# Two Strassen groups in the first FFN of an encoder kernel, with the tokens normalised in its middle

## The chip, the cores and the metric

The kernel runs on one core of a Trainium2 chip. The metric is device microseconds of one execution; the time of a version is the median of its runs. One execution is also taken with the hardware profiler, and all rows below come from that one. TensorE (PE) multiplies, VectorE (DVE) and ScalarE (ACT) do elementwise work, GpSimd (POOL) a few tiny things, and SP issues nearly all transfers from memory (DMA).

## The reference, cut to what matters

256 tokens of width 1024 go through two layers. Each layer is FFN, token mixing, FFN, every one with a norm before and after. All is float32.

```python
def rms_norm(x, g):
    xf = x * rsqrt(mean(x * x, axis=-1) + 1e-6)
    return xf * g

def swiglu(h, w_up, w_down):            # w_up 1024 x 5632, w_down 2816 x 1024
    a, b = split(h @ w_up, 2, axis=-1)
    return (silu(a) * b) @ w_down

for l in range(2):
    h = rms_norm(x, ffn1_pre_g[l])
    x = x + 0.5 * rms_norm(swiglu(h, ffn1_w_up[l], ffn1_w_down[l]), ffn1_post_g[l])
    x = x + rms_norm(mix(rms_norm(x, mix_pre_g[l]), mem, positions), mix_post_g[l])
    h = rms_norm(x, ffn2_pre_g[l])
    x = x + 0.5 * rms_norm(swiglu(h, ffn2_w_up[l], ffn2_w_down[l]), ffn2_post_g[l])
```

The mixing needs, among others, a cosine and sine table of the positions, a lambda from four small vectors, and memory tokens `mem`, normalised.

## The kernel before, in words

**Numbers in two parts.** A float32 matmul is made of three matmuls on parts: each operand is a high part (a rounded copy) and a low part (the rest). Products are high x high, high x low, low x high. Tokens and weights are both split so. For weights this is `split_unit` (lines 113 to 125): ScalarE copies the high part `wh` (line 119), VectorE subtracts to get the low part `wl` (line 120), each in two halves (four in the first five units of a stage).

**Units.** Weights lie in memory as units of 128 x 2048 floats, 1 MB, in the order of their use. SP loads them one after the other into five `raw` buffers; five `wh` and five `wl` buffers take the split ones. So loading and splitting run ahead of TensorE by as much as these buffers allow.

**An FFN** has 11 pairs, each 256 columns of the gate half and 256 of the value half of the up-weights. `up_both(p)` (`u` in the plan) takes two units and makes 48 matmuls of 128x512, 24 for each of the two token blocks (c = 0, 1) of 128 tokens. `swiglu` turns the bank into the hidden values, `turned` transposes them on TensorE (line 325) and splits them (lines 164, 165). `down(p)` (`d`) multiplies them by one unit of down-weights, 24 matmuls into the accumulators `acc` (line 277).

**A Strassen group** `group(p)` (`g`, line 384) makes two pairs together: four raw units w11, w12, w22, w21 (gate and value columns, upper and lower 512 rows), seven products of 12 matmuls on sums of weights (VectorE adds whole units, line 366) and sums of tokens (`token_sums`, line 374, from unsplit copies `kept` of the turned tokens). That is 84 matmuls instead of 96 for two plain pairs. VectorE and ScalarE split seven units instead of four.

**The plan** (line 37) is the order of an FFN, after pairs 0 and 1 and before the last three down-products. The second line is for the three later FFNs; the first line is for the first FFN, which has no groups: its tokens come raw. The host passes x also transposed, `first_tokens` multiplies it by the gain only, and the scale of each token, 1 / rms, is put on in `swiglu` (lines 337, 338). So the first product can start before the rms is known. Later stages get normalised tokens from `pre_norm` (line 187), whose `turn` transposes them (line 207) and splits them; copies go to `kept`.

**Other work inside the first FFN.** `ahead` (line 881), called after the sixth step of its plan (d2), runs `setup` (rope tables, lambda products; three small transfers, some 25 small VectorE operations, three sines), `mem_scale` (four transfers of mem, four squares, two scales) and `mem_gain` (four transfers of the transposed mem, split into the tile that the mixing reads). In layer 1 `ahead` runs `mem_gain` alone, after the whole plan.

**What sets the order.** The program is written in order of use, and a list scheduler places instructions on each engine: the earliest in the program that it takes to be ready goes next, and buffers are given out as earlier users release them. On the chip each engine keeps the order that was fixed then, and so does SP's queue of transfers. Pools that the change touches: `xhl` (split tokens, 2 buffers), `hid` (12), `s2` (8 of 128x512: swiglu values, kept tokens, setup's tables), `s4` (2), `gain` (2), and two banks each for `ma` and `mb`.

Of the kernel before, what the change touches and what calls it, by code (L numbers as in the profile page):

```python
# [9 lines left out]
F32 = mybir.dt.float32  # L10
F32R = mybir.dt.float32r
# [3 lines left out]
ALU = mybir.AluOpType  # L15
AX = mybir.AxisListType

P = 128
D = 1024
# [15 lines left out]
T_ROPE = 13  # L35
T_SC = (242, 336)
PLAN = [[(t[0], int(t[1:])) for t in plan.split()] for plan in (
    "u2 d0 u3 d1 u4 d2 u5 d3 u6 d4 u7 d5 u8 d6 u9 d7 u10",
    "u2 d0 g3 d1 d2 u5 d3 g6 d4 d5 u8 d6 g9 d7",
)]  # L40
T_KT = (200, 222)
# [10 lines left out]
def encoder_kernel(ctx, tc, x_d, xt_d, mem_d, memt_d, pos_d, w_d, gains_d, cols_d, lamv_d, poolw_d, cst_d, out_d):  # L52
    nc = tc.nc
# [20 lines left out]
    def mb_bank():  # L74
        return mmp.tile([P, 512], F32, name="mb")

    def t2(shape=(P, 512), dt=F32):
        return s2.tile(list(shape), dt, name="s2")
# [11 lines left out]
    def gain(row):  # L90
        g = gbp.tile([P, D], F32, name="gain")
        nc.sync.dma_start(out=g, in_=gains_d[row].partition_broadcast(P))
        return g
# [69 lines left out]
    def split(ps, h, l):  # L163
        high = nc.scalar.copy(out=h, in_=ps)  # L164
        return high, nc.vector.tensor_tensor(out=l, in0=ps, in1=h.bitcast(F32), op=ALU.subtract)  # L165
# [19 lines left out]
        return [gained_split((xx[0][:, c, 4 * b + k, :], xx[1][:, c, 4 * b + k, :]), t[:, k, :], colt[:, cols[k]:cols[k] + 1]) for k in range(4)]  # L185

    def pre_norm(c, src, g, xx, keep):
        xh, xl, _ = xx
        xn = s4.tile([P, D], F32, name="s4")

        def gained(var):
            for b in range(2):
                fs = slice(b * 512, (b + 1) * 512)
                issue_after([nc.vector.tensor_tensor(out=xn[:, fs], in0=src[b], in1=g[:, fs], op=ALU.mult)], var)

        r = rstd_of(src, 1.0, gained)
        for b in range(2):
            fs = slice(b * 512, (b + 1) * 512)
            nc.vector.tensor_scalar(out=xn[:, fs], in0=xn[:, fs], scalar1=r, scalar2=None, op0=ALU.mult)

        def turn():
            tps = []
            for b in range(2):
                ps = mb_bank()
                for k in range(4):
                    i = 4 * b + k
                    tps.append(nc.tensor.transpose(out=ps[:, k * P:(k + 1) * P], in_=xn[:, i * P:(i + 1) * P], identity=ident))  # L207
                pv = ps.rearrange("p (k t) -> p k t", t=P)
                split(pv, xh[:, c, b * 4:b * 4 + 4, :], xl[:, c, b * 4:b * 4 + 4, :])
                if keep is not None:  # L210
                    keep[c, b] = t2()
                    nc.scalar.copy(out=keep[c, b], in_=ps)
            return tps

        return turn

    def post_norm(c, banks, g, half_step):
        ts = [t2(), t2()]
# [77 lines left out]

    def ffn(i, xx, late, kept, g_post, finish, ahead, raw_rstd=None):
        fine[0] = FINE
        hid = {}
        acc = [[None, None], [None, None]]  # L300

# [31 lines left out]

        def swiglu(p, c, ps):
            sg, hn = t2((P, S)), t2((P, S))
            if raw_rstd:
                nc.scalar.activation(out=sg, in_=ps[:, 0:S], func=AF.Silu, scale=raw_rstd[c])
                nc.vector.scalar_tensor_tensor(out=hn, in0=ps[:, S:2 * S], scalar=raw_rstd[c], in1=sg, op0=ALU.mult, op1=ALU.mult)
            else:
                nc.scalar.activation(out=sg, in_=ps[:, 0:S], func=AF.Silu)  # L340
                nc.vector.tensor_tensor(out=hn, in0=ps[:, S:2 * S], in1=sg, op=ALU.mult)
            turned(hn, c, [p])
# [8 lines left out]
        def up_both(p):  # L351
            ws = (next_unit(), next_unit())
            for c in range(2):
                up(p, c, ws, leave=1 - c)
                if kept and p == 2 and c == 0:
                    token_sums()

        def product(out, at, w, first=True, last=True):
# [6 lines left out]
        def add(out, a, b):  # L365
            nc.vector.tensor_tensor(out=out, in0=a, in1=b, op=ALU.add)  # L366

        if kept:
            sums = xts.tile([P, 2, 4 * 4, P], F32R, name="xhl")

            def summed(j):
                return lambda k: (sums[:, 0, 4 * j + k, :], sums[:, 1, 4 * j + k, :])

        def token_sums():
            a11, a12, a21, a22 = (kept[c, b] for c in range(2) for b in range(2))
            s1 = t2()
            nc.vector.tensor_tensor(out=s1, in0=a22, in1=a21, op=ALU.subtract)
            nc.vector.tensor_tensor(out=a21, in0=a11, in1=a21, op=ALU.subtract)
            nc.vector.scalar_tensor_tensor(out=a11, in0=s1, scalar=-1.0, in1=a11, op0=ALU.mult, op1=ALU.subtract)
            nc.vector.scalar_tensor_tensor(out=a12, in0=a11, scalar=-1.0, in1=a12, op0=ALU.mult, op1=ALU.subtract)  # L380
            for j, t in enumerate((s1, a11, a21, a12)):
                split(t.rearrange("p (k t) -> p k t", t=P), sums[:, 0, 4 * j:4 * j + 4, :], sums[:, 1, 4 * j:4 * j + 4, :])
# [47 lines left out]
            for c in range(2):  # L430
                swiglu(p, c, banks[c])

        if raw_rstd:
            ws = [(next_unit(), next_unit())]
            hs, ls = first_high, first_low
            (ha, la), (hb, lb), (hc, lc), (hd, ld) = (zip(*late[c, b]) for b in range(2) for c in range(2))
            in_order([*ha, *hs[0:4], *hb, *hc, hs[4], hs[5], *hd, *hs[6:8]])
            in_order([*la, *ls[0:4], *lb, *lc, ls[4], ls[5], *ld, *ls[6:8]])
            ws.append((next_unit(), next_unit()))
            for c in range(2):  # L440
                rstd_of(halves(x[c]), 1.0, None, raw_rstd[c])
            up_first(0, ws[0])
            for c in range(2):
                up(1, c, ws[1], acc_bank)
        else:
            ws = [(next_unit(), next_unit()) for _ in range(2)]
            done = []
            for c in range(2):
                for p in range(2):
                    done += up(p, c, ws[p], acc_bank if c else ma_bank, 2)  # L450
            issue_after(late, done[T_UP])
        for n, (what, p) in enumerate(PLAN[bool(kept)]):
            if what == "d":
                down(p)
            elif what == "u":
                up_both(p)
            else:
                group(p)
            if not kept and n == 5:
                ahead()  # L460
        if kept:
            ahead()
        todo = [(next_unit(), p) for p in range(NPR - 3, NPR)]
        return tail(acc, todo, lhs_of, 0, NPR - 1, g_post, True, finish, flush)

# [103 lines left out]
    def mem_scale():  # L569
        for c in range(2):  # L570
            m = []
            for b in range(2):
                t = hids.tile([P, 512], F32, name="hid")
                nc.sync.dma_start(out=t, in_=mem_d[c * P:(c + 1) * P, b * 512:(b + 1) * 512])
                m.append(t)
            rstd_of(m, 1.0, None, rmem[:, c:c + 1])
# [269 lines left out]
    cur = xt_pair()  # L846
# [17 lines left out]
    kept = None  # L864
    for i, (kind, l, row) in enumerate(stages):
        nx = {}

        def finish(c):
            if i + 1 == len(stages):
                for b in range(2):  # L870
                    fs = slice(b * 512, (b + 1) * 512)
                    nc.sync.dma_start(out=out_d[c * P:(c + 1) * P, fs], in_=x[c][:, fs])
                return []
            if c == 0:
                nx["xx"] = xt_pair()
                nx["kept"] = {} if stages[i + 1][0] == "ffn" else None
                nx["g"] = gain(stages[i + 1][1] * 10 + stages[i + 1][2])
            return pre_norm(c, halves(x[c]), nx["g"], nx["xx"], nx["kept"])()

        if kind == "ffn":  # L880
            def ahead():
                if i == 0:
                    setup()
                    mem_scale()
                if row == 0:
                    nx["mem"] = mem_gain(l)

            late = ffn(i, cur, late, kept, gain(l * 10 + row + 1), finish, ahead, [rst[:, c:c + 1] for c in range(2)] if i == 0 else None)
        else:
            late = mix(l, cur, late, mem, finish)  # L890
        cur, mem, kept = nx.get("xx"), nx.get("mem"), nx.get("kept")
# [24 lines left out]
def _pack(a, np):  # L916
# [17 lines left out]
    def ffn(up, down, first):  # L934
        def pair(p):
            wide(up, np.r_[256 * p:256 * p + 256, D_FF + 256 * p:D_FF + 256 * p + 256])

        pair(0)
        pair(1)
        for what, p in PLAN[not first]:  # L940
            if what == "d":
                rows(down, p)
            elif what == "u":
                pair(p)
            else:
                for half, col in ((0, 0), (0, D_FF), (1, D_FF), (1, 0)):
                    block(up, half, 256 * p + col)
        for p in range(NPR - 3, NPR):
            rows(down, p)
# [59 lines left out]
```

## Time and profile before

| | |
|---|---|
| median of 3 runs | 1119.22 us (1118.71 to 1120.41) |
| the profiled execution | 1118.06 us, its span 1116.0 us |
| instructions | 13913 |
| TensorE clock granted | 0.998 of full speed |
| HBM read | 216.33 MB |

The stages in the profile, by the first matmul of each: first FFN 6 us, mixing 194, second FFN of layer 0 384, first FFN of layer 1 563, mixing 742, last FFN 932. A row of the timeline gives start, length, engine, line, operation, output <- inputs, shape and count; brackets hold the idle time of that engine just before and what ended it. PE is a matmul, PEld a load of weights into TensorE. Matmuls overlap, so the steps between their starts tell more than their lengths.

### The profile page before, as it was taken

What the parts mean: (1) busy time and instruction counts of PE and PEld (TensorE: products, weight loads), DVE (VectorE), ACT (ScalarE), POOL (GpSimd) and SP (SyncE); (2) the same over time, 40 slices, a digit from 0 to 9 for tenths busy, and PEclk for the clock granted to TensorE, in tenths of its full rate; (3) what the DMA queues carried; (4) which work ended last, traced back from release to release, by engine and by line L of the source; (5) the groups of instructions that cost most, each with busy time, mean ns of one, the idle gap of its engine ahead of it and who ended that gap; (6) DMA issues with size and microseconds to landing.
All of it is one profiled execution on the core that took longest, in us unless ns stands there. A gap on an engine that the chain in (4) does not pass through costs nothing.

```text
span 1116.0 us, 13913 instructions
## 1 busy us (share of the span) xinstructions
PE 1106.6 (99%) x5247; PEld 912.6 (82%) x5247; DVE 892.5 (80%) x1215; ACT 651.6 (58%) x1082; POOL 25.5 (2%) x37
## 2 busy tenths in 40 slices
PE   9999999999999999999999999999999999999997
PEld 6888888888888888888888888888888888888886
DVE  6767456657858899999989999995676678999994
ACT  7657345546575557474675674765566637575571
POOL 0000000000000100000000000010000001000000
PEclk9999999999999999999999999999999999999999
DMA  9966643564563454573851835565445645273731
GB/s 344 396 225 230 216 150 125 189 226 150 201 214 134 174 203 140 200 251 131 334 196 69 302 125 214 207 250 207 171 170 191 236 155 177 90 255 137 287 113 38
DMA packets 35489, 218.27 MB, mean 196 GB/s; under 512 B 4192, under 2 KB 4448, under 8 KB 11232
## 3 DMA queue, kind: packets, MB, share of 16 engines
q1 hardware_dynamic: 35424, 217.40, 53.6%
q8 instruction: 41, 0.67, 0.2%
q14 instruction: 24, 0.20, 0.0%
HBM read 216.33 MB, written 1.05 MB: 195 GB/s over the span
## 4 chain that ended last, share of the span: by engine, by line
PE 95%; DMA 2%; ACT 1%; DVE 1%; POOL 0%; issue 0%; SPq 0%; DVEq 0%; POOLq 0%; ACTq 0%
PE ma L235 52%; PE acc L277 24%; PE mb L235 9%; PE acc L235 5%; PE mb L325 2%; PE mb L207 1%; PE acc L664 1%; PE acc L687 1%; PE mb L564 1%; DMA hid<-in_memt 1%; DMA hid<-in_xt 1%; PE acc L750 1%; DMA raw<-in_w 0%; POOL sm L148 0%; PE acc L734 0%; DVE wl L120 0%
## 5 line engine op out<-in xcount | busy, mean ns | idle before, releaser
L120 DVE TENSOR_TENSOR wl<-raw,wh 128x1024 fp32r<-128x1024 f32 (+1 forms) x498 | 523.5, 1089 | 96.6 <-ACT wh L119 94.2
L119 ACT CAST wh<-raw 128x1024 fp32r<-128x1024 f32 (+1 forms) x498 | 444.4, 947 | 196.1 <-DVE raw L366 67.4
L235 PE MATMUL ma<-wh,xhl 128*128 128x512 f32 x1664 | 530.1, 393 | 0.1
L235 PEld LDWEIGHTS ma<-wh,xhl 128*128 128x128 f32 x1664 | 311.7, 188 | 65.5 <-issue 1.7
L235 PE MATMUL ma<-wl,xhl 128*128 128x512 f32 x832 | 327.1, 393 | 0.4 <-DVE wl L120 0.2
L277 PE MATMUL acc<-wh,hid 128*128 128x512 f32 x704 | 227.8, 395 | 0.0
L235 PEld LDWEIGHTS ma<-wl,xhl 128*128 128x128 f32 x832 | 156.4, 188 | 33.0 <-DVE wl L120 1.3
L277 PEld LDWEIGHTS acc<-wh,hid 128*128 128x128 f32 x704 | 132.2, 188 | 26.9
L277 PE MATMUL acc<-wl,hid 128*128 128x512 f32 x352 | 136.8, 390 | 0.0
L235 PE MATMUL mb<-wh,xhl 128*128 128x512 f32 x280 | 90.5, 389 | 0.0
L366 DVE TENSOR_TENSOR raw<-raw 128x2048 f32<-128x2048 f32 x36 | 82.2, 2284 | 0.4
L277 PEld LDWEIGHTS acc<-wl,hid 128*128 128x128 f32 x352 | 66.3, 188 | 12.7
L235 PEld LDWEIGHTS mb<-wh,xhl 128*128 128x128 f32 x280 | 52.6, 188 | 10.9
L235 PE MATMUL mb<-wl,xhl 128*128 128x512 f32 x140 | 54.5, 389 | 0.0
L235 PE MATMUL acc<-wh,xhl 128*128 128x512 f32 x160 | 51.6, 391 | 0.0
L340 ACT ACTIVATE s<-ma 128x256 f32<-128x256 f32 x24 | 8.9, 386 | 65.6 <-PE ma L235 65.2
L148 POOL TENSOR_TENSOR sm<-sm,mhalf 128x1 f32<-128x1 f32 (+1 forms) x26 | 22.6, 868 | 1002.3 <-DVE sm L157 822.8
L277 PE MATMUL acc<-wh,xhl 128*128 128x512 f32 x128 | 40.7, 394 | 0.0
L155 ACT ACTIVATE junk<-acc 128x512 bf16<-128x512 f32 x24 | 14.3, 597 | 44.1 <-PE acc L277 44.1
L164 ACT CAST hid<-mb 128x256 fp32r<-128x256 f32 x88 | 32.1, 370 | 13.1 <-PE mb L325 10.6
L165 DVE TENSOR_TENSOR hid<-mb,hid 128x256 fp32r<-128x256 f32 x88 | 36.3, 417 | 1.8 <-ACT hid L164 1.3
L235 PEld LDWEIGHTS acc<-wh,xhl 128*128 128x128 f32 x160 | 30.0, 188 | 6.2
(161 smaller groups left out, 880.5 us busy)
## 6 DMA issues: line engine op xcount, KB each, us to landing
raw<-in_w SPq DMA_DIRECT2D x189, 1024.0 KB, 4.8
gain<-in_gains SPq DMA_DIRECT2D x17, 512.0 KB, 4.7
raw<-in_w SPq DMA_DIRECT2D x8, 256.0 KB, 5.7
hid<-in_memt SPq DMA_DIRECT2D x8, 256.0 KB, 6.5
hid<-in_xt SPq DMA_DIRECT2D x4, 256.0 KB, 5.4
raw<-in_w SPq DMA_DIRECT2D x2, 512.0 KB, 7.0
x<-in_x SPq DMA_DIRECT2D x4, 256.0 KB, 6.6
hid<-in_mem SPq DMA_DIRECT2D x4, 256.0 KB, 9.3
```

What stands on the lines that cost most here:

```text
L119: high = nc.scalar.copy(out=h[:, cs], in_=raw[:, cs])
L120: low = nc.vector.tensor_tensor(out=l[:, cs], in0=raw[:, cs], in1=h.bitcast(F32)[:, cs], op=ALU.subtract)
L148: nc.gpsimd.tensor_tensor(out=r, in0=v, in1=mhalf[:, :n], op=ALU.pow)
L155: sq.append(nc.scalar.activation(out=junk, in_=h, func=AF.Square, scale=fold / 32.0, accum_out=s[:, i:i + 1]))
L164: high = nc.scalar.copy(out=h, in_=ps)
L165: return high, nc.vector.tensor_tensor(out=l, in0=ps, in1=h.bitcast(F32), op=ALU.subtract)
L207: tps.append(nc.tensor.transpose(out=ps[:, k * P:(k + 1) * P], in_=xn[:, i * P:(i + 1) * P], identity=ident))
L235: done.append(nc.tensor.matmul(out=out, lhsT=lhsT, rhs=rhs, start=(first and i == 0), stop=(last and i == n - 1)))
L277: done.append(nc.tensor.matmul(out=banks[b], lhsT=a, rhs=ww[:, k, fs], start=(kk == first and k == 0 and i == 0), stop=(kk == last and k = ...
L325: nc.tensor.transpose(out=tp[:, u * P:(u + 1) * P], in_=hn[:, u * P:(u + 1) * P], identity=ident)
L366: nc.vector.tensor_tensor(out=out, in0=a, in1=b, op=ALU.add)
L564: ins.append(nc.tensor.transpose(out=tp[:, i * P:(i + 1) * P], in_=a[:, hh, kt * P:(kt + 1) * P], identity=ident))
```

## The change

The first FFN gets its own kind of plan. Pairs 0 to 3 still run on raw x. Then step `n` (`normalised`) makes normalised tokens of the whole x: for each token block two fused multiplications (x times 1 / rms times gain) on VectorE, then the same transposes, splits and kept copies as `pre_norm` makes; the turning is now a function of its own, `turn_tokens`. The gains row 0 is loaded for it by SP. Step `s` makes the token sums and runs `setup`. From pair 4 on, `swiglu` works without the scale. Pairs 5 and 6 and pairs 8 and 9 become two groups; pairs 4, 7 and 10 stay plain. Step `m` is `mem_scale`, between d4 and u7. `ahead`, now only `mem_gain`, is called after the plan in every FFN. The host packs the units in the new order, by the same plan.

```diff
 PLAN = [[(t[0], int(t[1:])) for t in plan.split()] for plan in (
-    "u2 d0 u3 d1 u4 d2 u5 d3 u6 d4 u7 d5 u8 d6 u9 d7 u10",
+    "u2 d0 u3 n0 d1 s0 u4 d2 g5 d3 d4 m0 u7 d5 g8 d6 u10 d7",
     "u2 d0 g3 d1 d2 u5 d3 g6 d4 d5 u8 d6 g9 d7",
 )]
...
-        def turn():
-            tps = []
...
-            return tps
-
-        return turn
+        return lambda: turn_tokens(c, xn, xx, keep)
+
+    def turn_tokens(c, xn, xx, keep):
+        xh, xl, _ = xx
+        tps = []
+        for b in range(2):
+            ps = mb_bank()
+            for k in range(4):
+                i = 4 * b + k
+                tps.append(nc.tensor.transpose(out=ps[:, k * P:(k + 1) * P], in_=xn[:, i * P:(i + 1) * P], identity=ident))
+            pv = ps.rearrange("p (k t) -> p k t", t=P)
+            split(pv, xh[:, c, b * 4:b * 4 + 4, :], xl[:, c, b * 4:b * 4 + 4, :])
+            if keep is not None:
+                keep[c, b] = t2()
+                nc.scalar.copy(out=keep[c, b], in_=ps)
+        return tps
...
     def ffn(i, xx, late, kept, g_post, finish, ahead, raw_rstd=None):
         fine[0] = FINE
+        raw, sums = raw_rstd is not None, None
...
-            if raw_rstd:
+            if raw:
                 nc.scalar.activation(out=sg, in_=ps[:, 0:S], func=AF.Silu, scale=raw_rstd[c])
...
-                if kept and p == 2 and c == 0:
+                if not raw_rstd and p == 2 and c == 0:
                     token_sums()
...
-        if kept:
+        def normalised():
+            nonlocal xx
+            xx = xt_pair()
+            g = gain(0)
+            for c in range(2):
+                xn = s4.tile([P, D], F32, name="s4")
+                for fs in (slice(0, 512), slice(512, 1024)):
+                    nc.vector.scalar_tensor_tensor(out=xn[:, fs], in0=x[c][:, fs], scalar=raw_rstd[c], in1=g[:, fs], op0=ALU.mult, op1=ALU.mult)
+                turn_tokens(c, xn, xx, kept)
...
+        def token_sums():
+            nonlocal sums
             sums = xts.tile([P, 2, 4 * 4, P], F32R, name="xhl")
...
-        for n, (what, p) in enumerate(PLAN[bool(kept)]):
+        for what, p in PLAN[not raw]:
             if what == "d":
                 down(p)
             elif what == "u":
                 up_both(p)
+            elif what == "n":
+                raw = False
+                normalised()
+            elif what == "s":
+                token_sums()
+                setup()
+            elif what == "m":
+                mem_scale()
             else:
                 group(p)
-            if not kept and n == 5:
-                ahead()
-        if kept:
-            ahead()
+        ahead()
         todo = [(next_unit(), p) for p in range(NPR - 3, NPR)]
         return tail(acc, todo, lhs_of, 0, NPR - 1, g_post, True, finish, flush)
...
             def ahead():
-                if i == 0:
-                    setup()
-                    mem_scale()
                 if row == 0:
                     nx["mem"] = mem_gain(l)
...
-            late = ffn(i, cur, late, kept, gain(l * 10 + row + 1), finish, ahead, [rst[:, c:c + 1] for c in range(2)] if i == 0 else None)
+            late = ffn(i, cur, late, kept if i else {}, gain(l * 10 + row + 1), finish, ahead, [rst[:, c:c + 1] for c in range(2)] if i == 0 else None)
```

More of the change, by code (lines that the diff above doesn't have):

```diff
@@ L187, in pre_norm @@
     def pre_norm(c, src, g, xx, keep):
-        xh, xl, _ = xx
         xn = s4.tile([P, D], F32, name="s4")
@@ L199, in pre_norm @@
             nc.vector.tensor_scalar(out=xn[:, fs], in0=xn[:, fs], scalar1=r, scalar2=None, op0=ALU.mult)
-        def turn():
-            tps = []
[L203 to L212, printed above, removed]
-            return tps
-        return turn
+        return lambda: turn_tokens(c, xn, xx, keep)
[13 more added lines that the diff above has]
+        return tps
     def post_norm(c, banks, g, half_step):
@@ L366, in add, with summed @@
             nc.vector.tensor_tensor(out=out, in0=a, in1=b, op=ALU.add)
-        if kept:
+        def normalised():
[7 more added lines that the diff above has]
+                turn_tokens(c, xn, xx, kept)
+        def summed(j):
+            return lambda k: (sums[:, 0, 4 * j + k, :], sums[:, 1, 4 * j + k, :])
+        def token_sums():
+            nonlocal sums
             sums = xts.tile([P, 2, 4 * 4, P], F32R, name="xhl")
-            def summed(j):
-                return lambda k: (sums[:, 0, 4 * j + k, :], sums[:, 1, 4 * j + k, :])
-        def token_sums():
             a11, a12, a21, a22 = (kept[c, b] for c in range(2) for b in range(2))
@@ L431, in up_first @@
                 swiglu(p, c, banks[c])
-        if raw_rstd:
+        if raw:
             ws = [(next_unit(), next_unit())]
@@ L944, in ffn @@
                 pair(p)
-            else:
+            elif what == "g":
                 for half, col in ((0, 0), (0, D_FF), (1, D_FF), (1, 0)):
```

## The prediction

> **What bounds the kernel now.** I read the page's engine shares first, then the chain that ended last, then the timeline of single engines round the places the change touches.
>
> ```profile
> PE 1106.6 (99%) x5247; PEld 912.6 (82%) x5247; DVE 892.5 (80%) x1215; ACT 651.6 (58%) x1082; POOL 25.5 (2%) x37
> ...
> PE 95%; DMA 2%; ACT 1%; DVE 1%; POOL 0%; issue 0%; SPq 0%; DVEq 0%; POOLq 0%; ACTq 0%
> ```
>
> TensorE holds 95% of the chain of waits. A busy PE alone proves little, so the chain in order of time has to show that the matmuls follow each other at a fixed step (start, length, what; both in us):
>
> ```profile
> 48.02 10.92 PE ma L235 x48
> 59.16 5.45 PE acc L277 x24
> 64.84 10.92 PE ma L235 x48
> ...
> 81.67 10.91 PE ma L235 x48
> ...
> 424.67 2.75 PE ma L235 x12
> ...
> 472.41 2.77 PE ma L235 x12
> ...
> 491.50 2.72 PE acc L277 x12
> ...
> 503.35 10.88 PE ma L235 x48
> ```
>
> The first three rows are the first FFN: pair 3, down-product of pair 1, pair 4. A pair with a down-product takes 64.84 - 48.02 = 16.82 us, and 10.92 / 48 is 0.2275 us a matmul. The last three rows are the second FFN of layer 0, where a Strassen group (84 matmuls, two pairs at once) lasts 491.50 - 472.41 = 19.09 us, again 0.227 each. So TensorE is dense in both patterns, and a matmul less is 0.227 us less, as long as its weights are split in time.
>
> That condition is the second thing to read. Splitting is VectorE's work (the low halves, line 120), and a group adds whole weight units (line 366):
>
> ```profile
> L120 DVE TENSOR_TENSOR wl<-raw,wh 128x1024 fp32r<-128x1024 f32 (+1 forms) x498 | 523.5, 1089 | 96.6 <-ACT wh L119 94.2
> ...
> L366 DVE TENSOR_TENSOR raw<-raw 128x2048 f32<-128x2048 f32 x36 | 82.2, 2284 | 0.4
> ```
>
> Busy time by stretch (columns: length, then busy us and count of PE, PEld, DVE, ACT, POOL, clock, DMA share, GB/s): the pairs before the new first group, then a whole FFN with three groups.
>
> ```profile
> 48.00:82.00 34.00, 34.00 (x156) 28.01 (x155) 20.05 (x34) 17.28 (x26) 0.00 (x0) 1.00 0.72 263
> ...
> 384.00:562.60 178.60, 178.60 (x818) 147.80 (x817) 169.51 (x200) 110.06 (x165) 3.49 (x4) 1.00 0.57 206
> ```
>
> With groups VectorE is 169.51 / 178.60 = 95% busy; with plain pairs 20.05 / 34.00 = 59%. How little is left is seen just behind the first group of that FFN, at the down-product of pair 1, whose second low half is written and then read:
>
> ```profile
> 445.29 1.22 DVE L120 TENSOR_TENSOR wl<-raw,wh 128x1024 fp32r<-128x1024 f32 x1
> ...
> 446.55 0.39 PE L277 MATMUL acc<-wl,hid 128*128 128x512 f32 x1
> ```
>
> The write ends at 446.51 and the matmul starts at 446.55. I read this as no margin: whatever makes VectorE later inside a first group reaches TensorE in full.
>
> **The change, part by part.** Two groups replace four pairs. Per group and two down-products the old pattern takes 2 x 16.82 = 33.64 us, the new one 503.35 - 472.41 = 30.94, hid transposes included. That is 2.70 a group, **-5.40 us**.
>
> Normalising in the middle adds 16 token transposes. Eight of them, in the tail of the second FFN:
>
> ```profile
> 559.50 0.40 PE L277 MATMUL acc<-wh,hid 128*128 128x512 f32 x1
> 559.73 1.04 PE L207 MATMUL mb<-ident,s 128*128 128x128 f32 x8
> 560.52 0.48 PE L277 MATMUL acc<-wh,hid 128*128 128x512 f32 x1
> 560.83 0.39 PE L277 MATMUL acc<-wl,hid 128*128 128x512 f32 x1
> ```
>
> From 559.50 to 560.83 there are two matmuls and eight transposes: 1.33 - 0.45 = 0.88 us for eight, **+1.75 us** for sixteen, and the first group then starts at 81.67 + 1.75 = 83.4. [...] The busy time of the row above agrees with a long single one, but its eight start within 0.79 us, so I go by 0.11 each.
>
> The other new work of step n is four fused products on VectorE (0.68 us each by the row of line 379 below), which need only x, the first row of gains and the scale of each token, all there before pair 3 ends; four high and four kept copies on ScalarE, which is 17.28 / 34.00 busy; and four low halves on VectorE. Four turned banks share two PSUM buffers, so the second pair of banks waits for copies. Pair 1's down-product, 5.45 us, lies between; I charge nothing, with 0 to 1 us as the bounds.
>
> The sixteen token-sum operations and the setup of rope and lambda move ahead of the first group, where before the setup stood in the middle of plain pairs. Their prices, and how VectorE stood in each case ahead of a group:
>
> ```profile
> L165 DVE TENSOR_TENSOR xhl<-s,xhl 128x512 fp32r<-128x512 f32 x4 | 2.7, 684 | 0.1
> ...
> L379 DVE SCALAR_TENSOR_TENSOR s<-s,s 128x512 f32<-128x512 f32 x1 | 0.7, 683 | 0.0
> ```
>
> ```profile
> 57.34 2.36 DVE L120 TENSOR_TENSOR wl<-raw,wh 128x1024 fp32r<-128x1024 f32 x2 [2.74 <-ACT wh L119]
> ...
> 79.79 0.42 DVE L486 TENSOR_TENSOR s<-s 128x256 f32<-128x256 f32 x1
> ...
> 84.56 1.22 DVE L120 TENSOR_TENSOR wl<-raw,wh 128x1024 fp32r<-128x1024 f32 x1
> ...
> 87.25 0.18 DVE L523 COPY csd<-csd 128x16 f32<-128x16 f32 x1 [0.28 <-ACT csd L522]
> ```
>
> ```profile
> 405.33 2.36 DVE L120 TENSOR_TENSOR wl<-raw,wh 128x1024 fp32r<-128x1024 f32 x2
> ```
>
> ```profile
> 740.79 1.28 DVE L165 TENSOR_TENSOR xhl<-mb,xhl 128x512 fp32r<-128x512 f32 x2
> ```
>
> I take the second FFN as the pattern. There VectorE begins the group's first split at 405.33 and TensorE the group at 424.67: 19.3 us, in which VectorE also does the token sums. In the changed kernel the weights of pair 2's down-product, the last before the group, are split by 57.34 + 2.36 = 59.7; I take it that they cannot be earlier, since that row waited 2.74 us for the high half, which needs one of five buffers. From 59.7 to 83.4 are 23.7 us, 4.4 more than the pattern. But VectorE has more to do in them: the four low halves of step n, 4 x 0.64 = 2.6 us; the setup, from 79.79 to 87.43 is 7.6 us, of which 3.0 belongs to other work (a split half of 1.2, a memory split of 0.5 and six small ones of 0.2 to 0.4); less two hid splits of 0.4 that fall outside. 2.6 + 4.6 - 0.8 = 6.4, against 4.4. VectorE enters the group 2.0 us later than in the pattern, and with no margin **+2.0 us** is what TensorE waits. The bounds are 0 (the setup finds other gaps) and 2.0 + 2.7 = 4.7 (step n's four products fall into this stretch too), before anything that holds VectorE up. I keep 2.0, between them, because the products have idle time before 59.7 and the setup does not: its first operation needs a buffer and a transfer that come after step n.
>
> Queues. SP gets a gains row of 512 KB and the 304 KB constants earlier, while weights still come at the rate of the transfers, 263 GB/s and more in that stretch. 0.8 MB at 0.263 MB/us is 3.1 us; the weights of pair 1's down-product are split ten us before use (row below), which hides it. If that cover were gone, 3.1 us would show.
>
> ```profile
> gain<-in_gains SPq DMA_DIRECT2D x2, 512.0 KB, 7.9
> hid<-in_mem SPq DMA_DIRECT2D x4, 256.0 KB, 9.3
> hid<-in_memt SPq DMA_DIRECT2D x4, 256.0 KB, 7.0
> cst<-in_cst SPq DMA_DIRECT2D x1, 304.0 KB, 6.4
> s<-in_lamv SPq DMA_DIRECT2D x1, 256.0 KB, 9.1
> ```
>
> ```profile
> 44.11 4.63 DVE L120 TENSOR_TENSOR wl<-raw,wh 128x1024 fp32r<-128x1024 f32 x4 [0.44 <-ACT wh L119]
> ```
>
> These four halves end at 48.74, and the down-product starts at 59.16. The squares of mem (step m) are four operations of 0.6 us on ScalarE behind the group (row below), and ScalarE is 110.06 / 178.60 = 62% busy in an FFN with groups; nothing, and at most 2.4 us if ScalarE decided there.
>
> ```profile
> L155 ACT ACTIVATE junk<-acc 128x512 bf16<-128x512 f32 x24 | 14.3, 597 | 44.1 <-PE acc L277 44.1
> ```
>
> The memory tokens' transfers and splits move from the middle to the FFN's end. Layer 1 does this already, and shows a gap there:
>
> ```profile
> 738.08 0.61 PE L277 MATMUL acc<-wh,hid 128*128 128x512 f32 x2
> 738.79 0.88 DVE L199 TENSOR_SCALAR s<-s,sm 128x512 f32<-128x512 f32 x2 [0.44 <-POOL sm L148]
> 739.43 1.06 PE L207 MATMUL mb<-ident,s 128*128 128x128 f32 x8 [0.74 <-DVE s L199]
> ```
>
> 0.74 us, because VectorE reached the next normalisation late. The new plan ends with a plain pair and a down-product instead of a group, so there is more air: between 0 and 0.8, I take **+0.4**.
>
> Sum on the profiled execution: 1118.06 - 5.40 + 1.75 + 2.0 + 0.4 = 1116.8. The median of the runs, 1119.22, lies 1.16 above it, so the forecast is **1118.0 us**.
>
> **Rivals.** (a) *VectorE keeps its lead.* For it: 34.00 - 20.05 = 14 us of idle VectorE before the group, as much as the new work; the token sums are done before the group's weight additions, not among them as in the pattern. Against it: most of that idle time lies before the turned tokens exist. No stall gives 1114.4 profiled and 1115.6 as a median, with the tail's 0.4 1116.0.
>
> (b) *Slower: VectorE stands behind the lambda transfer.* VectorE runs in order, and setup's first product reads a 256 KB transfer that needs one of the eight s2 buffers. In the changed kernel four hold kept tokens, one the first sum and two or three pair 3's values, so the transfer starts when the sums release them. The copies are there near 65 (the transposes from 59.2 on, then four banks through ScalarE), eight VectorE operations of 0.68 us follow, so that is near 70.
>
> ```profile
> 69.31 0.42 SPq L481 DMA_DIRECT2D s<-in_lamv  x1
> ```
>
> It took 9.1 us to land (last column of its row above). Issued at 70 it lands at 79, while VectorE is through with the sums near 71: up to 8 us in which later splits queue behind that product, and the group's weights with them. From 3.5 us of such idleness on the kernel is slower by more than I could tell from no change; in the middle of 3.5 to 8, 1123 to 1124. Against it: in the kernel before, the product started at 79.79 right behind a split, without waiting, and its transfer was issued beside the gains row and the eight of mem, 2.5 MB, that no longer stand there.
>
> (c) *Transposes hold TensorE for 0.27 us each*, one after another: 16 x 0.27 = 4.3 instead of 1.75, so 1118.0 + 2.6 = 1120.6. Their mean duration speaks for it, their starts above against it.
>
> ```profile
> L207 PE MATMUL mb<-ident,s 128*128 128x128 f32 x80 | 10.4, 273 | 0.7 <-DVE s L199 0.7
> ```
>
> [...]
>
> **How the numbers follow.** I give the forecast 0.45, (a) 0.34, (b) 0.18, (c) 0.03. The forecast's own range, stalls of 1 to 4.7 us in all, is 1116.6 to 1120.3. The range for 8 in 10 takes in most of (a) and ends where (b) begins: 1115.2 to 1121.6. About 0.2%, 2.24 us, is what a measurement of this kernel tells from no change, so faster means below 1116.98: (a), and 0.02 of the forecast, 0.36. Slower means above 1121.46: (b), 0.18. The rest, 0.46, is within.
>
> **What would show it.** Fewer matmuls: 24 less of 128x512 in the first FFN and 16 more of line 207. Step right or wrong: the chain should show the first group stretched beyond 19.1 us or a wait for VectorE's low halves in it or the down-product behind it, about 2 us in all, and the second group dense. If both groups take 19.1 us, (a) holds. If VectorE idles before the lambda product, (b). If token transposes are 0.2 us apart, (c). A wait at pair 4's first matmuls would mean that the turning itself is late, and one at weights of pair 1 or 4 that the moved transfers are; either would make the accounting wrong.

## The result, and the profile after

The changed kernel takes 1122.18 us (median of 10 runs, 1120.68 to 1125.6) against 1119.38 for the kernel before beside it (10 runs, 1118.71 to 1120.41). The ratio is 1.0028, with a 95% interval of 1.0021 to 1.0036: **2.8 us slower**, where 1118.0 was forecast, and above the upper end of the range. The profiled execution took 1123.13 us, its span 1121.1 us, and so it lies 0.95 above its median; the profiled one of before lay 1.3 below its own. The profile therefore shows a larger difference (5.07) than the medians do.

The page's engine shares and the share of the chain of waits by engine, in the kernel after:

```profile
PE 1106.3 (99%) x5239; PEld 912.8 (81%) x5239; DVE 939.6 (84%) x1261; ACT 668.7 (60%) x1103; POOL 28.9 (3%) x37
...
PE 95%; DVE 3%; DMA 1%; ACT 1%; POOL 0%; issue 0%; SPq 0%; DVEq 0%; POOLq 0%; ACTq 0%
```

The change did what it says: 5239 matmuls instead of 5247 (24 fewer products, 16 more transposes), and 44 additions of whole weight units instead of 36. But TensorE is busy for the same 1106 us, with less work in it, and VectorE's share of the chain went from 1% to 3%. Both have to be found in the first FFN. The chain there, in order of time (start, length, what):

```profile
49.40 10.92 PE ma L235 x48
...
79.70 2.24 DVE raw L367
...
88.31 0.32 DVE s L526
88.63 0.34 DVE s L342
89.11 0.66 PE mb L326 x2
...
90.62 4.40 PE ma L235 x11
95.02 5.45 PE mb L235 x24
...
140.01 2.73 PE ma L235 x12
...
159.06 2.72 PE acc L277 x12
...
199.52 8.42 PE ma L235 x37
```

I take the stretch from pair 3's first matmul to the mixing's first long run of matmuls as the measure. Both rows stand in the chain of each kernel. After, it is 199.52 - 49.40 = 150.12 us. Before, the first row is the 48.02 quoted in the prediction, and the last one is this:

```profile
194.50 8.39 PE ma L235 x37
```

194.50 - 48.02 = 146.48. So 3.64 of the 5.07 us were lost in this stretch, and 1.38 before it, since pair 3 starts at 49.40 instead of 48.02 (taken up at the end).

Inside the stretch, the second group is what was forecast: 159.06 - 140.01 = 19.05 us. The first one is not, and the chain reaches it by way of VectorE: a weight addition (L367), a rope operation of the setup (L526), and then L342. L342 is the product of pair 4's swiglu. TensorE then transposes that product (L326). The timelines of TensorE, ScalarE and VectorE at this place:

```profile
84.27 0.39 PE L277 MATMUL acc<-wh,hid 128*128 128x512 f32 x1
89.11 0.66 PE L326 MATMUL mb<-ident,s 128*128 128x128 f32 x2 [4.45 <-DVE s L342]
...
90.85 1.05 PE L235 MATMUL ma<-wh,xhl 128*128 128x512 f32 x2
91.70 0.63 PE L235 MATMUL ma<-wl,xhl 128*128 128x512 f32 x1
```

```profile
82.06 3.89 ACT L119 CAST wh<-raw 128x1024 fp32r<-128x1024 f32 x4 [3.35 <-DVE s L514]
...
87.26 0.38 ACT L341 ACTIVATE s<-ma 128x256 f32<-128x256 f32 x1
```

```profile
77.05 0.42 DVE L501 TENSOR_TENSOR s<-s 128x256 f32<-128x256 f32 x1
...
88.54 0.42 DVE L342 TENSOR_TENSOR s<-ma,s 128x256 f32<-128x256 f32 x1
```

Two losses can be read here. First, **a wait**: TensorE is through with pair 2's down-product at 84.27 + 0.23 = 84.5 and starts the transposes of pair 4 at 89.11, 4.6 us later. Pair 4's own matmuls had ended before that down-product, which is 24 matmuls or 5.45 us long, so by 79.1. Its Silu came only at 87.26 on ScalarE and its product at 88.54 on VectorE, behind nearly the whole setup. ScalarE's load is not what held that Silu: the engine stood idle for 3.35 us up to 82.06, and from 79.1 on at the latest the Silu's input was there. Second, **slow matmuls behind the wait**: from 90.62 to 95.02 eleven matmuls take 4.40 us, 0.40 each where 0.227 is the rule. The stretch by time shows why (columns as in the prediction; the clock is the third number from the end):

```profile
88.90:95.00 6.10, 5.89 (x17) 4.83 (x18) 6.10 (x13) 1.96 (x5) 0.00 (x0) 0.54 0.47 172
```

After the idle 4.6 us the granted clock is 0.54 for some 6 us; the next 24 matmuls, from 95.02 on, take 5.45 us, 0.227 each, at a clock of 1.00. From 89.11 on there are four transposes and the twelve matmuls of the group's first product, and the next one starts at 94.86: 5.75 us, where 4 x 0.11 + 12 x 0.227 = 3.2 would do. The clock costs 2.6 us. That also explains TensorE's busy time, since slow matmuls count as busy: 5.89 of the 6.10 us in the row above, at the clock of 0.54.

So the account of the stretch, in profiled times, is -3.5 (the change without these two, measured below) + 4.6 + 2.6 = +3.7, and 3.64 was seen.

### The profile page after: what moved, and what is told of

It is laid out like the page before. It is cut to its first block, busy times and chain, and to the rows that moved or that the text cites. A ratio compares the mean times of both kernels' runs of the same rounds, so it can differ in the third digit from the quotient of the medians.

```text
span 1121.1 us, 13972 instructions
## 1 busy us (share of the span) xinstructions
PE 1106.3 (99%) x5239; PEld 912.8 (81%) x5239; DVE 939.6 (84%) x1261; ACT 668.7 (60%) x1103; POOL 28.9 (3%) x37
## 4 chain that ended last, share of the span: by engine, by line
PE 95%; DVE 3%; DMA 1%; ACT 1%; POOL 0%; issue 0%; SPq 0%; DVEq 0%; POOLq 0%; ACTq 0%
PE ma L235 50%; PE acc L277 23%; PE mb L235 10%; PE acc L235 5%; PE mb L326 2%; DVE wl L120 1%; PE mb L209 1%; PE acc L679 1%; PE acc L702 1%; DMA hid<-in_memt 1%; PE mb L579 1%; PE acc L765 1%; DMA raw<-in_w 0%; DVE raw L367 0%; POOL sm L148 0%; PE acc L749 0%
## 5 line engine op out<-in xcount | busy, mean ns | idle before, releaser
L120 DVE TENSOR_TENSOR wl<-raw,wh 128x1024 fp32r<-128x1024 f32 (+1 forms) x510 | 539.2, 1095 | 72.9 <-ACT wh L119 70.4
L119 ACT CAST wh<-raw 128x1024 fp32r<-128x1024 f32 (+1 forms) x510 | 456.6, 950 | 192.9 <-DVE raw L367 68.0
L235 PE MATMUL ma<-wh,xhl 128*128 128x512 f32 x1600 | 512.9, 394 | 1.4 <-ACT wh L119 1.4
L235 PEld LDWEIGHTS ma<-wh,xhl 128*128 128x128 f32 x1600 | 301.3, 189 | 64.7 <-ACT wh L119 2.2
L235 PE MATMUL ma<-wl,xhl 128*128 128x512 f32 x800 | 315.9, 395 | 0.2 <-DVE wl L120 0.2
L235 PE MATMUL mb<-wh,xhl 128*128 128x512 f32 x328 | 105.9, 389 | 0.0
L367 DVE TENSOR_TENSOR raw<-raw 128x2048 f32<-128x2048 f32 x44 | 100.6, 2287 | 0.5
L235 PEld LDWEIGHTS mb<-wh,xhl 128*128 128x128 f32 x328 | 61.6, 188 | 12.8
L235 PE MATMUL mb<-wl,xhl 128*128 128x512 f32 x164 | 63.8, 389 | 0.0
L235 PEld LDWEIGHTS mb<-wl,xhl 128*128 128x128 f32 x164 | 30.8, 188 | 6.4
```

The costliest lines, as they stand in the source:

```text
L119: high = nc.scalar.copy(out=h[:, cs], in_=raw[:, cs])
L120: low = nc.vector.tensor_tensor(out=l[:, cs], in0=raw[:, cs], in1=h.bitcast(F32)[:, cs], op=ALU.subtract)
L235: done.append(nc.tensor.matmul(out=out, lhsT=lhsT, rhs=rhs, start=(first and i == 0), stop=(last and i == n - 1)))
```

## The experiments

Three theories of the slower time were put to the chip. **Q**: pair 4's swiglu product stands behind the setup, because the setup's tables and the swiglu's values come from the same eight `s2` buffers, given out in the order of the program; four hold kept tokens. **W**, the prediction's: VectorE has too much work ahead of the first group, wherever the product stands. **N**: the turning of the tokens and their sums are what comes late. What is compared is the stretch from pair 3 to the mixing; the kernel before was profiled a second time to see how far two executions of one code differ in it (last experiment).

### setup_late: the setup to the end of the FFN

```diff
-    "u2 d0 u3 n0 d1 s0 u4 d2 g5 d3 d4 m0 u7 d5 g8 d6 u10 d7",
+    "u2 d0 u3 n0 d1 s0 u4 d2 g5 d3 d4 m0 u7 d5 g8 d6 r0 u10 d7",
...
             elif what == "s":
                 token_sums()
+            elif what == "r":
                 setup()
```

> The setup of rope and lambda runs behind d6 instead of with the token sums; nothing else is moved. Theory Q (pair 4's swiglu product stands behind setup on VectorE, TensorE waits 4.6 us for it, and then runs some 12 matmuls at half clock, 2.7 us): the wait at 84 us and the slow matmuls go, so 1122.2 - 7.3, 1114.5 to 1116.5. Theory W (the prediction's: VectorE has too much to do before the group): 4.6 us of work less than the 2.0 it was late, no wait either, the same time. Rival N (the turning and the token sums are what is late, setup is not): the wait stays, about 1122.

1115.39 us (10 runs) against 1119.54; ratio 0.9967 (0.9958 to 0.9976). It is **4.2 us faster than the kernel before** and 6.8 faster than the change, so it beats both. Its chain and the product in VectorE's timeline:

```profile
48.43 10.92 PE ma L235 x48
...
84.18 2.75 PE ma L235 x12
...
103.25 2.73 PE acc L277 x12
...
191.41 8.42 PE ma L235 x37
```

```profile
76.08 0.42 DVE L342 TENSOR_TENSOR s<-ma,s 128x256 f32<-128x256 f32 x1
```

The product runs 12.5 us earlier, TensorE meets no wait, and the first group lasts 103.25 - 84.18 = 19.07 us. The stretch is 191.41 - 48.43 = 142.98, 3.50 less than before. The prediction's first two terms alone give -5.40 + 1.75 = -3.65. Moving the setup away takes away its buffers and its VectorE time at once, though, so this run speaks for Q or W alike; it only clears N, since the turning and the sums stand where they stood.

### setup_own: the setup in place, in other buffers

The setup's tables go into three `hid` buffers (of which there are twelve). Its place in the program and its work stay the same.

```diff
-        lv = t2((P, DEPTH, 2, 2, 64))
+        lv = hids.tile([P, DEPTH, 2, 2, 64], F32, name="hid")
+        ha, hb = hids.tile([P, 512], F32, name="hid"), hids.tile([P, 512], F32, name="hid")
...
-        prod = t2((P, DEPTH, 2, 64))
+        prod = ha[:, 0:256].rearrange("p (l i d) -> p l i d", l=DEPTH, i=2)
...
-        ang = t2((P, 2, 8))
+        ang = hb[:, 0:16].rearrange("p (c f) -> p c f", c=2)
...
-        tmp = t2((P, 240))
+        tmp = ha[:, 256:496]
```

> Setup stays where the change puts it and does the same work, but its tables lie in three hid buffers instead of s2 buffers, so pair 4's swiglu need not wait until setup gives buffers back. Theory Q with buffers as its cause: the product of pair 4 stands ahead of most of setup, the wait at 84 us goes, 1115 to 1117.5. Theory W: the same work in the same stretch, so the wait moves into the group or the down-product behind it, some 2 us and more: 1117 to 1120. If neither buffers nor setup matter (N): about 1122.

1116.53 us (10 runs) against 1119.54; ratio 0.9975 (0.9964 to 0.9985). Its chain, then ScalarE's and VectorE's timelines:

```profile
49.31 10.92 PE ma L235 x48
...
84.92 2.75 PE ma L235 x12
...
192.77 8.41 PE ma L235 x37
```

```profile
74.88 0.39 ACT L341 ACTIVATE s<-ma 128x256 f32<-128x256 f32 x1
```

```profile
65.46 0.41 DVE L502 TENSOR_TENSOR hid<-hid 128x256 f32<-128x256 f32 x1
...
80.90 0.43 DVE L342 TENSOR_TENSOR s<-ma,s 128x256 f32<-128x256 f32 x1
...
83.96 0.41 DVE L527 TENSOR_TENSOR hid<-hid 128x240 f32<-128x240 f32 x1
```

This is the run that decides. Most of the setup still stands ahead of the first group (L527, L526 of the change, at 83.96), yet the Silu comes at 74.88 instead of 87.26 and both products are done by 81.33. VectorE is busy for 32.75 of the 35.50 us from 49.40 to 84.90, and TensorE all the same starts the group without a wait. The stretch is 143.46 us, 0.48 more than in setup_late. So of the price of the setup's place, the buffers made nearly all: Q holds, and W is not what made TensorE wait. Two limits belong to this. With buffers that are free early the setup itself also starts earlier (L502, the lambda product, at 65.46 instead of 77.05), so the run shows what the buffers cost, through the swiglu and through the setup's start together. And the 0.48 us for VectorE's time comes from one execution of each kernel; by the medians the two are 1.14 us apart, with ranges that overlap (1114.49 to 1118.9 and 1113.91 to 1118.28).

The profiled execution itself took 1118.85 us, 2.3 above its median. Part of that lies in a place that the change doesn't touch, the end of layer 1's first FFN:

```profile
738.87 1.43 PE L209 MATMUL mb<-ident,s 128*128 128x128 f32 x8 [1.92 <-DVE s L198]
```

That wait was 0.74 us in the kernel before. Behind it the granted clock is 0.61 from 738.8 to 743.2, where it was 0.54 behind the wait in the change.

### s_behind_u4: pair 4 ahead of sums and setup

```diff
-    "u2 d0 u3 n0 d1 s0 u4 d2 g5 d3 d4 m0 u7 d5 g8 d6 u10 d7",
+    "u2 d0 u3 n0 d1 u4 s0 d2 g5 d3 d4 m0 u7 d5 g8 d6 u10 d7",
```

> Token sums and setup stand behind pair 4 in the program instead of before it. Theory Q: pair 4's product is free, so no wait of 4.6 us for it; what is left is that sums and setup stand right ahead of the group. Theory W: the sums are late for the group's second product, and VectorE's whole work before the group is unchanged, so a wait of 2 to 5 us stands in the group: 1117 to 1121. Rival N: about 1122, with the wait for pair 4's turn still there.

1119.23 us against 1119.54; ratio 1.0 (0.9989 to 1.0012): no change from the kernel before. The swiglu now gets its buffers first, and the wait ahead of the group is gone. Four of the group's products, 48 matmuls, run without a wait; the fifth one to run stands behind the setup. (The second product, which W expected to wait for the token sums, starts on time at 87.67.) From the chain and from TensorE's timeline:

```profile
93.45 2.21 DVE raw L367
...
98.28 4.45 PE ma L235 x12
...
196.40 8.42 PE ma L235 x37
```

```profile
87.67 0.39 PE L235 MATMUL mb<-wh,xhl 128*128 128x512 f32 x1
...
95.60 0.39 PE L235 MATMUL ma<-wh,xhl 128*128 128x512 f32 x1
98.28 0.79 PE L235 MATMUL ma<-wh,xhl 128*128 128x512 f32 x1 [2.29 <-ACT s L405]
```

The chain goes through a weight addition (L367) and its high half on ScalarE. TensorE is idle for 2.46 us (95.82 to 98.28), and twelve matmuls then take 4.45 us instead of 2.72. Here VectorE's work does bind, as W has it, because sums and setup now stand nearer to the additions. Its price is 2.5 + 1.7 us, and -3.5 + 4.2 = +0.7 is near the +0.58 of its stretch (196.40 - 49.34 = 147.06).

### norm_only: the normalisation without groups

Tokens are normalised behind pair 3 as in the change; all pairs stay plain, no token sums are made, and the setup stands behind d2. All of the computation is there.

```diff
-    "u2 d0 u3 n0 d1 s0 u4 d2 g5 d3 d4 m0 u7 d5 g8 d6 u10 d7",
+    "u2 d0 u3 n0 d1 u4 d2 r0 m0 u5 d3 u6 d4 u7 d5 u8 d6 u9 d7 u10",
```

> Plain pairs only: step n after u3 as in the change, but no token sums and no groups; setup and mem_scale stand behind d2 as before, the memory tokens at the end as in the change. All theories: +1.75 us for 16 transposes over the kernel before, 1121.1, plus 0 to 0.8 at the FFN's end. Rival N: the turning itself makes TensorE wait at pair 4, then 2 us more, 1123.

1121.2 us against 1119.54: +1.66 us, ratio 1.0017 (1.0007 to 1.0026). The prediction charged 1.75 for the sixteen transposes. In the chain and in TensorE's timeline:

```profile
48.92 10.92 PE ma L235 x48
...
60.06 0.44 PE mb L209 x4
...
198.33 8.39 PE ma L235 x37
```

```profile
194.51 0.39 PE L277 MATMUL acc<-wl,hid 128*128 128x512 f32 x1
195.64 1.06 PE L209 MATMUL mb<-ident,s 128*128 128x128 f32 x8 [0.74 <-DVE s L198]
```

Four transposes take 0.44 us, 0.11 each; the four rows of this kind in the chain are 0.44, 0.44, 0.58 and 0.44, together 1.90 us. In the profiled execution the stretch is 149.41, 2.93 longer than before; about 0.9 of that is a gap at the tail (194.51 + 0.23 to 195.64), where TensorE waits for the next normalisation, and the rest, 2.0, is near the 1.90. The change and setup_late don't have this gap. Since it stands in the 1.66 of the medians too (interval 0.8 to 2.9), the chain's 1.90 is the better measure of the transposes.

### keep_clock: matmuls in the place of the idle time

26 bf16 matmuls of 384 columns on zeros are put behind pair 2's down-product. Their result is not read. The transposes of pair 4 wait as in the change.

```diff
+        def keep_busy(n):
+            ps = mb_bank()
+            for _ in range(n):
+                dummies.append(nc.tensor.matmul(out=ps[:, 0:384], lhsT=busy[:, 0:P], rhs=busy, start=True, stop=True))
...
+                if raw_rstd and p == 4 and c == 0:
+                    keep_busy(N_BUSY)
```

> The changed kernel with 26 bfloat16 matmuls of 384 columns added on TensorE behind pair 2's down-product, where it waits 4.6 us for pair 4; they multiply zeros and nothing reads their result. If the half clock of the dozen matmuls behind the wait comes from TensorE having stood idle, they run at 0.23 us instead of 0.43 and about 2.7 us come back: 1119.5. If the slow matmuls have another cause (operands, a shared port), nothing comes back: 1122 or a little above.

1120.19 us, where 1119.5 was expected, against 1119.53; ratio 1.0005 (0.9995 to 1.0014), **2.0 us less than the change**. TensorE's timeline, its chain and a stretch of it (its lines are shifted by a few):

```profile
83.97 4.40 PE L320 MATMUL mb<-busy 128*128 128x384 bf16 x26
88.59 0.41 PE L340 MATMUL mb<-ident,s 128*128 128x128 f32 x2 [0.22 <-DVE s L356]
```

```profile
89.81 2.30 PE ma L238 x10
```

```profile
88.50:95.00 6.50, 6.41 (x30) 5.17 (x31) 6.50 (x14) 4.31 (x9) 0.00 (x0) 1.00 0.45 161
```

The transposes still come 39.7 us after pair 3's start, as in the change (88.59 - 48.91, 89.11 - 49.40), so the wait is the same. But the clock in the stretch behind it is 1.00 instead of 0.54, and ten matmuls take 2.30 us. That separates the two losses: the clock is 2.0 us by the medians, 2.4 by the two profiled stretches (196.64 - 48.91 = 147.73 against 150.12), and 2.6 by the count of slow matmuls above.

### setup_early: the setup ahead of the normalisation

```diff
-    "u2 d0 u3 n0 d1 s0 u4 d2 g5 d3 d4 m0 u7 d5 g8 d6 u10 d7",
+    "u2 d0 r0 u3 n0 d1 s0 u4 d2 g5 d3 d4 m0 u7 d5 g8 d6 u10 d7",
```

> Setup stands behind d0, ahead of pair 3, where VectorE is 59% busy; the rest as in the change. Theory Q: its s2 buffers are free again before the kept tokens need theirs, pair 4's product is not held up: 1115 to 1116.5, like setup behind d6. If the lambda transfer or the 0.6 MB of setup's transfers delay the weights there (they come at the transfer rate until 46 us): 1 to 3 us above that.

1117.0 us (9 runs), half a microsecond above what Q gave it, against 1119.53; ratio 0.9976 (0.9966 to 0.9986). The first and last rows of the stretch:

```profile
48.46 10.91 PE ma L235 x48
...
191.79 8.44 PE ma L235 x37
```

143.33 us, 3.15 less than before. With the setup in front, where the `s2` buffers are not yet held by kept tokens, most of the gain is there as well, as Q has it.

### three_groups: a third group, normalised one pair earlier

```diff
-    "u2 d0 u3 n0 d1 s0 u4 d2 g5 d3 d4 m0 u7 d5 g8 d6 u10 d7",
+    "u2 n0 d0 s0 d1 g3 d2 u5 d3 g6 d4 m0 d5 u8 d6 g9 d7 r0",
```

> Three groups: only pairs 0 to 2 on raw x, step n behind pair 2, groups at 3, 6 and 9, setup behind d7. Without waits -3 x 2.70 + 1.75 = -6.35 us against the kernel before, 1113.2. VectorE has the token sums close ahead of the first group, so a wait of 1 to 5 us there: 1114 to 1118, and then no better than setup_late's 1115.4.

1130.76 us (4 runs) against 1119.53; ratio 1.01 (1.0085 to 1.0115), 11 us slower, although it has 12 matmuls less than the change. It is far outside the 1114 to 1118 that were expected. Its stretch from 40 to 95 us, its longest wait there (place, releaser: idle us, how often, longest), a row of the chain, and TensorE at the FFN's end:

```profile
40.00:95.00 55.00, 49.02 (x212) 38.96 (x212) 50.56 (x56) 33.55 (x47) 0.00 (x0) 0.94 0.47 171
```

```profile
ACT wh L119 <- DVE raw L367: 8.3, 2, 4.8
```

```profile
78.58 4.37 PE mb L235 x11
```

```profile
202.17 1.94 PE L209 MATMUL mb<-ident,s 128*128 128x128 f32 x8 [2.96 <-DVE s L198]
```

VectorE is busy 50.56 of 55.00 us; ScalarE's high halves wait 8.3 us for VectorE's sums of weights, and TensorE for both (its matmuls into `mb` 2.4 us for the high halves and 2.2 for the low ones), so that it is busy 49.02. In two rows of the chain the matmuls are slow: eleven in 4.28 us, from 65.53 on, and eleven in 4.37, the row shown; that is 0.39 and 0.40 each instead of 0.227. Here VectorE is the bound in earnest. But this is not the whole loss: at the FFN's end, where the setup now stands beside the memory tokens, TensorE waits for 2.96 and, at 211.28, for 1.89 us more, and its clock is 0.79 from 200 to 215. The run changes both places at once, so it does not price the third group alone.

### before_again: the kernel before, once more

> The kernel before, unchanged, for its first 13 us once more. If the slow matmuls in the first 13 us, seen in most profiles of the changed kernels and not in the one of before, belong to the execution and not to the change, they may stand here as well; if they belong to the change, the first matmul is at 6.1 us and all run at 0.23 us again.

1119.24 us, span 1117.0. From its chain:

```profile
47.62 10.92 PE ma L235 x48
...
194.33 8.39 PE ma L235 x37
```

Its stretch is 194.33 - 47.62 = 146.71 us against 146.48 in the first profile. Two executions of the same code agree there to 0.23 us, which is what the differences between stretches above can be held against.

## Why the prediction was wrong

**Right: the groups, -5.40.** In setup_late the first group takes 19.07 us, in the change the second one 19.05, against 19.09 taken from the second FFN. With the transposes as forecast, the sum of the two terms is -3.65; with the 1.90 of norm_only's chain it is -3.50, and setup_late's stretch shows -3.50.

**Right: the transposes, +1.75.** norm_only has them without groups; they take 1.90 us in its chain, and it costs 1.66 us by the medians. With that, rival (c), 0.27 each, is out; the starts told the truth, not the mean duration.

**Right: what was charged at nothing.** The turned banks' PSUM buffers, the moved transfers and the squares of mem show no wait of TensorE in the chains of the change and of setup_late. The tail's +0.4 was 0 in the change and in setup_late, and 0.9 in norm_only (0.74 by its bracket); the bounds (0 to 0.8) were about right.

**Wrong: "VectorE enters the group 2.0 us later than in the pattern, and with no margin +2.0 us is what TensorE waits."** Both halves of this step failed. *The quantity*: I added up VectorE's work and asked when the group's weights would be split. In setup_own the same work stands in the same place of the program, and TensorE starts the group without a wait and loses 0.48 us against setup_late. There VectorE's lateness was worth some 0.5 us, not 2.0; the idle time of 14 us that rival (a) counted took most of the work up. In the change itself the group starts 4.6 us late, which hides what VectorE would have cost behind it, and in s_behind_u4 TensorE did wait 2.46 us for VectorE inside the group. So the worry was sound for some orders; the sum of busy time could not tell for which. *The place*: what came late was not the weights but pair 4's swiglu, two short instructions on ScalarE and VectorE, ahead of which the setup had been put; what came of it was 4.6 us of waiting, where 2.0 stood in the sum. An engine's busy sum cannot show that. The prediction counted the `s2` buffers (four kept tokens, one sum, pair 3's values) but asked only for the setup's sake who must give one back; it did not go one step on and ask who takes buffers *after* the setup. That next one is pair 4's swiglu. Which of the eight buffers it waited for, the trace does not say.

**Missed altogether: the clock.** The price of a wait was taken as its length. Here 4.6 us of idle TensorE cost another 2 to 2.6 us, shown by keep_clock, in which the wait stays and the slow matmuls don't. With 0.5 in the place of 2.0 and 0 in that of 0.4 the forecast would have been 1116.1; setup_own, which has neither the wait nor the slow matmuls at the first group, measured 1116.53.

**The sign of rival (b), not its mechanism.** (b) said slower, 1123 to 1124, because VectorE would stand behind the lambda transfer issued near 70. The transfer was issued at 61.49:

```profile
61.49 0.42 SPq L496 DMA_DIRECT2D s<-in_lamv  x1
```

The product that reads it (L501, quoted above) ran at 77.05; no idle time stands before it. That the time came out near (b)'s is no merit of (b); its thought of a scarce buffer was the right one, on the wrong consumer.

**Open: the start.** 1.38 us of the profiled difference arise before pair 3. The first stretch of after:

```profile
6.00:12.50 6.50, 4.87 (x13) 3.61 (x14) 4.99 (x15) 5.58 (x14) 0.00 (x0) 0.75 0.98 344
```

The first matmuls of the change run at a clock of 0.75 on average, those of before at 1.00, with 24 of them in the stretch instead of 13. The program text of that part is the same in all runs but for one memset in keep_clock; pair 3 starts at 48.43 in setup_late, 48.91 in keep_clock, 49.31 in setup_own and 49.34 in s_behind_u4. The clock is not the whole of it, since norm_only starts pair 3 at 48.92 with a clock of 1.00, and the two profiles of before differ by 0.40 us (48.02 and 47.62). Whether it is chance or something that the later plan moves was not settled; against these two profiles it is worth 1.4 to 1.8 us. It is not in the stretches compared, but it is in every median.

## What to carry to other kernels

When work that nobody waits for is moved ahead of work that somebody waits for, look at the pools that both take buffers from, and ask who is next in line for each one; adding up the busy time of the engine answers another question. Giving the moved work buffers of its own, or another place, was worth 5.2 to 6.8 us here, more than the change itself was to bring. And price a wait on TensorE with the slow matmuls behind it: here the one of 4.6 us cost another 2.0 to 2.6 us by them, the one of 2.46 us in s_behind_u4 another 1.7.

## What the runs showed of the hardware

I had not expected that a single wait in the middle of dense work would be followed by a lower granted clock, as it was here. After 4.6 us of idleness the clock was 0.54 over the next 6.1 us, with matmuls 0.43 us apart at first (90.85, two matmuls, 91.70). The wait of 2.46 us in s_behind_u4 did the same: from 98.28 on twelve matmuls took 4.45 us, with steps of 0.23 us again from 101.42 on. So did the one in layer 1 of setup_own, 1.92 us by its bracket: the clock was 0.61 from 738.8 to 743.2. At the same place in before_again the bracket is 1.29 us, and the matmuls behind it stayed at 0.23 us. With unread matmuls in the gap, in keep_clock, the clock was 1.00 from 83.9 to 95.0.

Full steps came back 3.1 us behind the wait in s_behind_u4, 4.1 in setup_own and 5.5 in the change. The gaps of 2.46 and of 1.92 us that slow matmuls followed were seen in one profiled execution each.
